# A decoder step on one core: the feed-forward stage's fp32r weight splits replaced by fp16 splits with scales found on the chip

## The chip, the cores and the metric

The kernel runs on one core of one Trainium2 chip. The metric is the device time of one execution in microseconds (us); lower is better. The kernel before takes 1934.26 us, the median of 3 runs (1932.78 to 1934.76).

Five engines of the core matter here. PE multiplies matrices: it holds a block of 128 x 128 weights (loaded by an LDWEIGHTS, shown as PEld) and streams columns of the activations past it into PSUM. DVE, ACT and POOL work element by element. SP only issues DMAs here. Each engine works through its own instructions in a fixed order and waits, where it must, for the others.

## The reference

One step of a one-layer decoder trunk on 256 prompt tokens and 8 x 4 sample tokens, so N = 288 columns; the model width is 2048 (16 blocks of 128, `KT`) and the hidden width of the feed-forward stage is 8192. Only the end of it bears on the change:

```python
mix, st = mixer(xn, states[l], P)
x = x + gt1 * mix
xn = rmsnorm(x, P['g_norm2']) * (1.0 + sc2) + sh2
x = x + gt2 * (jnp.square(jax.nn.relu(xn @ P['w_ff1'])) @ P['w_ff2'])
...
y = rmsnorm(x, g_final)
```

`sh2`, `sc2` and `gt2` are pieces of `mod = silu(c) @ w_ada + b_ada`, one row for the prompt and one for each of the 8 samples (9 columns). All of it is float32, and the weights come from HBM as float32.

## The kernel before

Activations lie transposed: features on the 128 partitions, the 288 tokens along the row. Every large product (the input projection, the branches, `wout`, `wf1`, `wf2`) goes through one generator, `stream` (L151). A weight matrix is cut into blocks of output columns (512 wide); each block is read in tiles of 128 x 1024 floats (512 KB, two row groups of 128 by 512 columns). For each tile:

- SP issues the load of `raw`;
- ACT copies it to `hi`, rounded to fp32r, the type with which PE makes a matmul of 4-byte numbers in one pass (L159);
- DVE makes `lo = raw - hi` (L161);
- PE runs, for each 128 x 128 piece, three matmuls with 288 moving columns: hi by xh, hi by xl and lo by xh (L168), where xh and xl are the same split of the activations. That is 24 matmuls per tile.

A block accumulates in four PSUM banks and is then evacuated by the function `evac` that the caller gives.

The feed-forward stage runs over 8 hidden blocks `hb` of 1024 features. `ff1(hb)` (L1752) makes 1024 hidden features from all 2048 inputs: 2 blocks of `wf1` with 16 row groups each, so 192 matmuls per block of 512 columns. Each result goes through Relu on ACT (L1757), a square on POOL (L1758) and a split into hi and lo on ACT and DVE (L575, L576). `ff2(hb)` (L1764) multiplies these 1024 features with their rows of `wf2`: 4 blocks of 96 matmuls, added to `facc` by DVE (L1774); with hb 6 and 7 the residual with `gt2` follows (L1692 to L1697). The order in the program is ff1(0), then for each hb: ff1(hb+1), ff2(hb). So what ff1(hb+1) makes is not needed by the block that PE does right after it, but four blocks later. Together the stage has 6144 matmuls of 288 columns.

Ahead of it stands a norm: the `wout` blocks end, `every("")` finishes leftovers of the adaLN product (L300), the sum of squares becomes `rs` (L536, L557 to L561), and a loop over 16 features (L1740 to L1746) makes xh2 and xl2: DVE scales (L1740), ACT rounds (L1741, L1744), DVE and POOL subtract.

The remaining adaLN work (`gt2`) runs beside the stage in an order given by a string, `every("E L . L ...")`: at each step of `run` a letter loads, transforms or multiplies one unit of `wada`. Its matmuls have 32 stationary columns (L300 plain fp32, L361 fp16 on scaled parts); four of them use the four column groups of the array at once.

Instructions that are issued under `tc.high_priority()` are put ahead of others on their engine, and a scheduler fixes the order of each engine when the program is built.

Of the kernel before, what the change touches and what calls it, by code (L numbers as in the profile page):

```python
# [8 lines left out]
F32 = mybir.dt.float32  # L9
# [45 lines left out]
def trunk(ctx, tc, io):  # L55
# [22 lines left out]
    def slot(i, dt=F32):  # L78
        return big.tile([P, 8, N], dt, tag=f"s{i}", name=nm(f"s{i}"))
# [28 lines left out]

    ones = cp.tile([P, P], F32, tag="ones", name="ones")
    V.memset(ones, 1.0)  # L110
    eps = cp.tile([P, 1], F32, tag="eps", name="eps")
    V.memset(eps, EPS)

# [37 lines left out]
    def stream(w, blk, act, kt, evac, g0=0, width=512, ahead=True, k0=0, kg=2, behind=None, banks=None):  # L151

        nm_t = width // P
        pss = banks or [pm.tile([P, 512], F32, tag="mm", name=nm("mm")) for _ in range(nm_t)]
        for g in range(k0 // kg, kt // kg):
            with tc.high_priority() if ahead else nullcontext():
                raw, hi, lo = (t.rearrange("p (k m) -> p k m", k=kg) for t in weight_tiles())
                Q.dma_start(raw, w[blk, g0 + g].rearrange("p (k m) -> p k m", k=kg))
                pace["hi"] = S.activation(hi, raw, AF.Copy)  # L159
                with tc.issue_after(behind.ins) if behind and g == 0 else nullcontext():  # L160
                    pace["lo"] = V.tensor_tensor(out=lo, in0=raw, in1=hi.bitcast(F32), op=ALU.subtract)  # L161

            def part(m, kk, i):
                k = kg * g + kk
                ps, ms = pss[m][:, :N], slice(m * P, (m + 1) * P)
                xh, xl = act(k)
                w, x = ((hi, xh), (hi, xl), (lo, xh))[i]
                pace["last"] = T.matmul(ps, w[:, kk, ms], x, start=k == k0 and i == 0, stop=k == kt - 1 and i == 2)  # L168

            if behind and g == 0:  # L170
                for i in range(3):
                    for kk in range(kg):
                        for m in range(nm_t):
                            with tc.issue_after(pace["last"].ins) if pace["last"] else nullcontext():
                                part(m, kk, i)
                yield
                continue
            if behind and g == 1:
                for m in range(nm_t):
                    for kk in range(kg):  # L180
                        for i in range(2):
                            with tc.issue_after(pace["last"].ins):
                                part(m, kk, i)
            for m in range(nm_t):
                for kk in range(kg):
                    for i in range(2 if behind and g == 1 else 0, 3):
                        part(m, kk, i)
                if g == kt // kg - 1:
                    with tc.high_priority():
                        evac(m, pss[m][:, :N])  # L190
            yield


# [1514 lines left out]
    for b in range(4):  # L1708
        def ev_o(m, p, b=b):
            k = 4 * b + m  # L1710
            x = x2[k // 8][:, k % 8, :]
            resid(x, p, GT1, k)
            if k == KT - 1:
                with tc.high_priority(), tc.issue_after(pace["last"].ins):
                    visit(4)
                with tc.issue_after(pace["prod"].ins):
                    sumsq(pss, x, k, ssum)
                with tc.high_priority(), tc.issue_after(pace["sum"].ins):
                    visit()
            else:  # L1720
                sumsq(pss, x, k, ssum)
            if k == KT - 4:
                S.activation(sc([P, 1], "warm", 1), ssum[:, 0:1], AF.Sqrt)
        if b == 3:
            drain("sm1")
            xf.extend((slot(6), slot(7)))
# [6 lines left out]
    xh2 = big.tile([P, KT, N], F32R, tag="xh", name="xh2")  # L1733
    xl2 = big.tile([P, KT, N], F32R, tag="xl", name="xl2")
    with tc.high_priority():
        for k in range(KT):
            f = row(("ar", "mr")[k % 2])
            E = V if k < 2 else G
            h, l, sh = xh2[:, k, :], xl2[:, k, :], mod[:, SH2, k, 0:1]
            V.tensor_tensor(out=f, in0=xf[k // 8][:, k % 8, :], in1=rs, op=ALU.mult)  # L1740
# [4 lines left out]
            V.scalar_tensor_tensor(l[:, 0:NP], f[:, 0:NP], sh, h[:, 0:NP].bitcast(F32), ALU.add, ALU.subtract)  # L1745
            E.tensor_tensor(out=l[:, NP:N], in0=f[:, NP:N], in1=h[:, NP:N].bitcast(F32), op=ALU.subtract)  # L1746


    facc = (slot(6), slot(7))
    pss = None  # L1750

    def ff1(hb):  # L1752
        hh, hl = slot(hb % 2, F32R), slot(2 + hb % 2, F32R)
        for b in range(2):
            def ev(m, p, b=b):
                r = t288()
                S.activation(r, p, AF.Relu)  # L1757
                G.tensor_tensor(out=r, in0=r, in1=r, op=ALU.mult)  # L1758
                i = 4 * b + m
                split(hh[:, i, :], hl[:, i, :], r)  # L1760
            run(stream(io["wf1"], 2 * hb + b, ahead=hb + b > 0, act=lambda k: (xh2[:, k, :], xl2[:, k, :]), kt=KT, evac=ev))
        return hh, hl

    def ff2(hb, h):  # L1764
        for b in range(4):
            def ev(m, p, b=b):
                k = 4 * b + m
                a = facc[k // 8][:, k % 8, :]
                if hb == 0:
                    S.copy(a, p)  # L1770
                    return
                x = x2[k // 8][:, k % 8, :]
                if hb < 7:
                    V.tensor_tensor(out=a, in0=a, in1=p, op=ALU.add)  # L1774
                    if hb == 6:
                        resid(x, a, GT2, k)
                    return
                resid(x, p, GT2, k)
# [3 lines left out]
            run(stream(io["wf2"], b, lambda k: (h[0][:, k, :], h[1][:, k, :]), 8, ev, g0=4 * hb))  # L1782

    h = ff1(0)
    at.update(raw=(None, None, 8))
    slots.update(ids=(9, None, "st"), n=0)
    high.update(ids=(None,))
    every("E L . L . L . . C C C C C C C C C C C C V . .")
    for hb in range(8):
        hn = ff1(hb + 1) if hb < 7 else None  # L1790
        if hb == 6:
# [134 lines left out]
```

## Time and profile before

| what | value |
|---|---|
| median of 3 runs | 1934.26 us |
| span of the profiled execution (first to last instruction) | 1929.9 us |
| feed-forward stage, first to last L168 matmul | 1093.16 to 1915.3 us |
| PE busy over the span | 99% |
| DVE, ACT, POOL busy over the span | 59%, 48%, 12% |
| mean granted clock of TensorE | 0.998 |

The profiled execution's own time is not listed beside its span; the median of the runs is 4.4 us longer than the span, and these 4.4 us are taken as what lies around it. In a row of the groups, "L161 DVE ... x448 | 553.5, 1237" means 448 instructions of line 161, busy for 553.5 us together, 1237 ns each. A row of the timeline gives start, length and a number of neighbouring instructions of one form. For pipelined matmuls the length of one (about 290 ns) is a latency; what PE can do is read from start to start.

### The profile page before, as it was taken

How to read it: one execution, taken by the hardware profiler on the slowest of the kernel's cores; microseconds unless marked ns; L12 is line 12 of the kernel's file. 1: busy time of each engine (PE TensorE's matmuls, PEld its weight loads, DVE VectorE, ACT ScalarE, POOL GpSimd, SP SyncE). 2: the span in 40 equal slices, each digit the busy share in tenths (PEclk: the TensorE clock that was granted, in tenths of full speed). 3: DMA queues.
4: the chain of work that ended last, by engine and by line, in shares of the span. 5: the costliest groups of instructions: out<-in, count | busy, mean ns of one | idle time of the engine just before them, and what ended most of it. 6: DMA issues, size and time to landing. Idle time of an engine off the chain costs nothing.

```text
span 1929.9 us, 37907 instructions
## 1 busy us (share of the span) xinstructions
PE 1902.8 (99%) x15792; PEld 1834.5 (95%) x15792; DVE 1135.2 (59%) x1833; ACT 922.9 (48%) x1361; POOL 238.5 (12%) x315
## 2 busy tenths in 40 slices
PE   8999999999999999999999999999999999999997
PEld 7998888999999999999999999999999999999997
DVE  4677746545684457776478756456454444454565
ACT  5333464444455344566377547465333333343433
POOL 0002100001141000011113521010000000000101
PEclk9999999999999999999999999999999999999999
DMA  9998756547744369856787564654444445444442
GB/s 388 394 367 313 249 197 235 208 161 269 257 154 159 132 217 313 302 186 242 282 349 280 186 243 147 241 198 161 164 167 167 165 154 181 167 165 165 162 169 111
DMA packets 113436, 422.85 MB, mean 219 GB/s; under 512 B 11808, under 2 KB 12096, under 8 KB 110064
## 3 DMA queue, kind: packets, MB, share of 16 engines
q1 hardware_dynamic: 97040, 361.04, 52.5%
q0 software_dynamic: 11472, 42.79, 6.3%
q10 hardware_dynamic: 4752, 16.60, 2.1%
q8 instruction: 124, 2.03, 0.4%
q14 instruction: 48, 0.39, 0.1%
HBM read 403.56 MB, written 16.81 MB: 218 GB/s over the span
## 4 chain that ended last, share of the span: by engine, by line
PE 93%; DVE 4%; DMA 1%; ACT 1%; issue 1%; DVEq 0%; POOL 0%; ACTq 0%; POOLq 0%
PE mm L168 82%; PE pa L300 3%; PE px L168 2%; DVE lo L161 1%; DMA raw<-win 1%; PE pa L361 1%; DVE s L728 0%; PE px L1577 0%; ACT hi L159 0%; PE pi L1560 0%; PE px L1095 0%; PE px L1491 0%; DMA s<-x 0%; PE px L817 0%; DVE s L672 0%
## 5 line engine op out<-in xcount | busy, mean ns | idle before, releaser
L161 DVE TENSOR_TENSOR lo<-raw,hi 128x1024 fp32r<-128x1024 f32 x448 | 553.5, 1237 | 486.3 <-ACT hi L159 465.9
L159 ACT ACTIVATE hi<-raw 128x1024 fp32r<-128x1024 f32 x448 | 473.7, 1059 | 700.7 <-PE mm L168 537.8
L168 PE MATMUL mm<-xh,hi 128*128 128x288 f32 x2464 | 725.9, 299 | 4.1 <-ACT xh L646 1.7
L168 PE MATMUL mm<-xl,hi 128*128 128x288 f32 x2464 | 722.8, 296 | 0.0
L168 PE MATMUL mm<-xh,lo 128*128 128x288 f32 x2464 | 706.6, 295 | 2.0 <-DVE lo L161 1.9
L168 PE MATMUL mm<-s,hi 128*128 128x288 f32 x3328 | 655.9, 296 | 1.1 <-DVE s L1697 0.7
L168 PEld LDWEIGHTS mm<-s,hi 128*128 128x128 f32 x3328 | 527.1, 188 | 5.3 <-issue 3.1
L168 PEld LDWEIGHTS mm<-xh,hi 128*128 128x128 f32 x2464 | 460.3, 188 | 17.0 <-issue 8.6
L168 PE MATMUL mm<-s,lo 128*128 128x288 f32 x1664 | 471.1, 295 | 1.6 <-DVE lo L161 1.0
L168 PEld LDWEIGHTS mm<-xl,hi 128*128 128x128 f32 x2464 | 462.3, 188 | 1.4
L168 PEld LDWEIGHTS mm<-xh,lo 128*128 128x128 f32 x2464 | 456.6, 188 | 4.9 <-DVE lo L161 2.9
L168 PEld LDWEIGHTS mm<-s,lo 128*128 128x128 f32 x1664 | 306.5, 188 | 2.3 <-DVE lo L161 2.1
L161 DVE TENSOR_TENSOR lo<-s,hi 128x1024 fp32r<-128x1024 f32 x80 | 98.0, 1224 | 102.6 <-ACT hi L159 102.6
L159 ACT ACTIVATE hi<-s 128x1024 fp32r<-128x1024 f32 x80 | 84.8, 1061 | 127.3 <-PE mm L168 124.0
L1758 POOL TENSOR_TENSOR t<-t 128x288 f32<-128x288 f32 x64 | 64.4, 1020 | 637.2 <-ACT t L1757 637.2
L1774 DVE TENSOR_TENSOR s<-s,mm 128x288 f32<-128x288 f32 x96 | 40.0, 449 | 28.4 <-PE mm L168 27.4
L1258 POOL TENSOR_TENSOR s<-s,t 128x288 f32<-128x288 f32 x16 | 22.6, 1441 | 169.3 <-DVE t L1257 135.9
L576 DVE TENSOR_TENSOR s<-t,s 128x288 fp32r<-128x288 f32 x64 | 32.4, 546 | 15.5 <-ACT s L575 15.5
L575 ACT ACTIVATE s<-t 128x288 fp32r<-128x288 f32 x64 | 27.5, 442 | 25.6 <-POOL t L1758 25.6
L300 PE MATMUL pa<-s,silc 128*32 128x128 f32 (+2 forms) x768 | 33.9, 322 | 1.0 <-DMA s<-wq 1.0
L300 PEld LDWEIGHTS pa<-s,silc 128*32 128x32 f32 x768 | 22.4, 115 | 9.8 <-issue 6.6
L168 PE MATMUL px<-xh,hi 128*128 128x288 f32 x96 | 28.3, 300 | 0.0
(473 smaller groups left out, 1477.0 us busy)
## 6 DMA issues: line engine op xcount, KB each, us to landing
raw<-win SPq DMA_DIRECT2D x192, 512.0 KB, 4.5
raw<-wf SPq DMA_DIRECT2D x176, 512.0 KB, 4.3
s<-wf SPq DMA_DIRECT2D x80, 512.0 KB, 3.5
s<-wq SPq DMA_DIRECT2D x20, 1024.0 KB, 9.8
raw<-wout SPq DMA_DIRECT2D x32, 512.0 KB, 5.8
s<-wada SPq DMA_DIRECT2D x13, 1024.0 KB, 7.6
ag<-wada POOLq DMA_DIRECT2D x12, 1024.0 KB, 7.5
ag<-wada SPq DMA_DIRECT2D x11, 1024.0 KB, 6.5
```

The source lines that it names most:

```text
L159: pace["hi"] = S.activation(hi, raw, AF.Copy)
L161: pace["lo"] = V.tensor_tensor(out=lo, in0=raw, in1=hi.bitcast(F32), op=ALU.subtract)
L168: pace["last"] = T.matmul(ps, w[:, kk, ms], x, start=k == k0 and i == 0, stop=k == kt - 1 and i == 2)
L300: pace["prod"] = T.matmul(ps[32 * j:32 * j + 32, h * w // 4:(h + 1) * w // 4], stat(k), v[:, j], start=k == 0 and h == 0, stop=k == kt - 1 ...
L361: pace["prod"] = T.matmul(ps[32 * j:32 * j + 32, a:a + 256], c, v[:, j], start=q == i == n == 0, stop=q == KT // each - 1 and n == 1, skip ...
L575: S.activation(dst_h[:, r], src[:, r], AF.Copy)
L576: V.tensor_tensor(out=dst_l[:, r], in0=src[:, r], in1=dst_h[:, r].bitcast(F32), op=ALU.subtract)
L1258: (V if br == 1 else G).tensor_tensor(out=a, in0=a, in1=t, op=ALU.add)
L1758: G.tensor_tensor(out=r, in0=r, in1=r, op=ALU.mult)
L1774: V.tensor_tensor(out=a, in0=a, in1=p, op=ALU.add)
```

## The change

In the feed-forward stage only, `stream` is replaced by `stream_half`, which works with fp16:

- **The scale of a block.** Each block has 4 raw tiles and 96 matmuls. ACT squares each raw tile with a running sum per partition (L235), PE adds the 128 partitions by a small matmul with ones (L238), and DVE turns the sum into powers of two u and t by integer arithmetic on the exponent (`power_of_two`, four instructions on 128 x 1, L198 to L201), then `c = t * back` (L241).
- **The split.** hi = u times raw, rounded to fp16, by ACT for every other tile (L247) and by DVE for the others (L249); lo = u times raw minus hi, in fp16, by DVE (L250). The matmuls (L258) are all fp16.
- **The blocks.** `wf1` comes in 256-wide blocks, so ff1 has 4 blocks of 96 matmuls where it had 2 of 192.
- **The activations.** x is scaled through SC2 and SH2 (ahead of the last `wout` block) and split into fp16 (`x16`). In ff1 the evacuation is Relu with scale c on ACT (L1841) and a square on ACT with row sums (L1842); POOL has nothing left to do there. At the end of ff1 the row sums go through ACT (L1847), a matmul with ones (L1849) and `power_of_two`, and only then is the hidden block split into fp16, in four pieces of 128 x 576 on ACT (L1854) and DVE (L1855).
- **The evacuation of ff2** multiplies by c (L1871).
- **Buffers.** 11 raw tiles in rotation (three of them `raw`, four parts of one tile `xl`, two of `s8`, two of `s3`) and 6 pairs of hi and lo. The string of `every` is spaced anew.

The core of the diff (line numbers of the changed kernel are those named above):

```diff
+    def power_of_two(p, n, of):
+        q, t, u = (of[:, i:i + 1] for i in (4, 5, 6))
+        V.tensor_reduce(out=q, in_=p[:, 0:n], axis=AX.X, op=ALU.add)
+        V.tensor_scalar(q.bitcast(I32), q.bitcast(I32), 0x7F000000, 1, ALU.bitwise_and, ALU.logical_shift_right)
+        V.tensor_scalar(u.bitcast(I32), q.bitcast(I32), -1, 204 << 23, ALU.mult, ALU.add)
+        V.tensor_scalar(t.bitcast(I32), q.bitcast(I32), 50 << 23, None, ALU.add)
+        return t, u
...
+    def stream_half(w, blk, act, kt, evac, back, g0=0, width=512):
...
+        with tc.high_priority():
+            for g in range(n):
+                raw = half_raw()
+                Q.dma_start(raw, w[blk, g0 + g])
+                pace["hi"] = S.activation(junk, raw, AF.Square, accum_out=of[:, g:g + 1])
+                raws.append(raw)
+            p = misc()
+            T.matmul(p[:, 0:n], words(ones, 1, BF16), words(of[:, 0:n], 1, BF16), start=True, stop=True)
+            t, u = power_of_two(p, n, of)
+            c = of[:, 7:8]
+            V.tensor_tensor(out=c, in0=t, in1=back, op=ALU.mult)
+        for g in range(n):
+            with tc.high_priority():
+                hi, lo = half_pair()
+                half["n"] += 1
+                if half["n"] % 2:
+                    pace["hi"] = S.activation(hi, raws[g], AF.Copy, scale=u)
+                else:
+                    V.tensor_scalar(hi, raws[g], u, None, ALU.mult)
+                pace["lo"] = V.scalar_tensor_tensor(lo, raws[g], u, hi, ALU.mult, ALU.subtract)
...
+    half["raw"] = ["raw", "raw", "raw"] + [("xl", i, 64) for i in range(4)] + [("s8", i, 32) for i in range(2)] + [("s3", i, 32) for i in range(2)]
...
     def ff1(hb):
-        hh, hl = slot(hb % 2, F32R), slot(2 + hb % 2, F32R)
-        for b in range(2):
-            def ev(m, p, b=b):
+        h = slot(2)
+        rows = sc([P, 8], "lam6", 1)
+        for b in range(4):
+            def ev(m, p, c, b=b):
+                i = 2 * b + m
                 r = t288()
-                S.activation(r, p, AF.Relu)
-                G.tensor_tensor(out=r, in0=r, in1=r, op=ALU.mult)
-                i = 4 * b + m
-                split(hh[:, i, :], hl[:, i, :], r)
+                S.activation(r, p, AF.Relu, scale=c)
+                S.activation(h[:, i, :], r, AF.Square, accum_out=rows[:, i:i + 1])
...
+        with tc.high_priority():
+            hof = sc([P, 8], "hs", 2)
+            q = hof[:, 0:1]
+            S.activation(rows, rows, AF.Square, accum_out=q)
+            p = misc()
+            T.matmul(p[:, 0:1], ones, q, start=True, stop=True)
+            back, u = power_of_two(p, 1, hof)
+            hx = big.tile([P, 2, 8, N], F16, tag=f"s{hb % 2}", name=nm("hx"))
+            for i in range(0, 8, 2):
+                r = slice(i, i + 2)
+                S.activation(hx[:, 0, r], h[:, r], AF.Copy, scale=u)
+                V.scalar_tensor_tensor(hx[:, 1, r], h[:, r], u, hx[:, 0, r], ALU.mult, ALU.subtract)
+        return hx, back
```

The order of the instructions is the same before and after until just ahead of the last `wout` block. Two engines are shown behind it, both at the end of one ff1, where ff2's first block begins.

PE before, the last matmuls of an ff1 (stationary hi or lo, moving xh2 or xl2) and the first of the ff2 that follows (moving s0 and s2, the hidden block made earlier):

```order
L168 MATMUL mm_2469_18077<-xl2_12669,hi_2492_18289 128x288
L168 MATMUL mm_2469_18077<-xh2_12668,lo_2493_18290 128x288
L168 MATMUL mm_2498_18338<-s0_2302_16766,hi_2503_18343 128x288
L168 MATMUL mm_2498_18338<-s2_2303_16767,hi_2503_18343 128x288
L168 MATMUL mm_2498_18338<-s0_2302_16766,lo_2504_18344 128x288
```

PE after, the same place (px: a PSUM bank for the small sums; hs: the row sums of the hidden block; sums: the sums of a block's raw tiles; x16: the scaled activations; lo_2360 and hi_2374 are pairs of hi and lo halves):

```order
L258 MATMUL mm_2352_18451<-x16_12678,lo_2360_18551 128x288
L1849 MATMUL px_2364_18586<-hs_2363_18584,ones_87 128x1
L238 LDWEIGHTS ones_87
L238 MATMUL px_2373_18616<-sums_2370_18605,ones_87 128x4
L238 LDWEIGHTS ones_87
L238 MATMUL px_2386_18751<-sums_2382_18739,ones_87 128x4
L258 LDWEIGHTS hi_2374_18623
L258 MATMUL mm_2366_18601<-hx_2260_17461,hi_2374_18623 128x288
```

Where one block's matmuls ran into the next one's, three sums now stand between them: that of the hidden block just finished, and behind it those of the next two blocks of weights. The other seven ends of an ff1 read the same.

DVE before, at the same place: the lo parts of the last tiles of ff1 and of the first tiles of ff2 (lo_2504 is the first that ff2 uses), with the splits of the hidden block (s3) among them:

```order
L161 TENSOR_TENSOR lo_2490_18260<-s8_2488_18258,hi_2489_18259 128x1024
L161 TENSOR_TENSOR lo_2493_18290<-raw_2491_18288,hi_2492_18289 128x1024
L161 TENSOR_TENSOR lo_2504_18344<-raw_2502_18342,hi_2503_18343 128x1024
L161 TENSOR_TENSOR lo_2507_18374<-s8_2505_18372,hi_2506_18373 128x1024
L576 TENSOR_TENSOR s3_2433_17809<-t288_2494_18300,s1_2432_17808 128x288
L161 TENSOR_TENSOR lo_2510_18404<-raw_2508_18402,hi_2509_18403 128x1024
```

DVE after, from the moment the next block's scale u is known (a pair, hi half and lo half, is one buffer here, and the buffers are called hi and lo in turn: hi_2374 is the pair that ff2's first matmuls use, lo_2375, lo_2377 and lo_2388 are other pairs of the next two blocks; L249 writes a pair's hi half, L250 its lo half):

```order
L249 TENSOR_SCALAR lo_2377_18704<-s3_2372_18613,sums_2370_18605 128x1024
L200 TENSOR_SCALAR sums_2382_18739<-sums_2382_18739 128x1
L201 TENSOR_SCALAR sums_2382_18739<-sums_2382_18739 128x1
L241 TENSOR_TENSOR sums_2370_18605<-sums_2370_18605,hs_2258_17453 128x1
L1855 SCALAR_TENSOR_TENSOR hx_2365_18592<-s2_2312_18045,hs_2363_18584,hx_2365_18592 128x576
L250 SCALAR_TENSOR_TENSOR lo_2375_18650<-s8_2371_18608,sums_2370_18605,lo_2375_18650 128x1024
...
L250 SCALAR_TENSOR_TENSOR lo_2377_18704<-s3_2372_18613,sums_2370_18605,lo_2377_18704 128x1024
L249 TENSOR_SCALAR lo_2388_18785<-raw_2383_18742,sums_2382_18739 128x1024
L241 TENSOR_TENSOR sums_2382_18739<-sums_2382_18739,hs_2258_17453 128x1
...
L250 SCALAR_TENSOR_TENSOR hi_2374_18623<-xl_2355_18456,sums_2370_18605,hi_2374_18623 128x1024
```

The lo part that ff2 needs first (the last row) moved behind those of other pairs, and behind three of the four pieces of the hidden block's split (L1855; two of them are at the "..." marks). Ahead of the first row shown stand ten small instructions of three `power_of_two` and one more L249. ACT's order there is: Relu and square of ff1's last results (L1841, L1842), in seven of the eight places one more L235, then L1847, three L1854, and the L247 of pair hi_2374.

More of the change, by code (lines that the diff above doesn't have):

```diff
@@ new lines, in trunk, with half_raw, half_pair @@
+    half = {"raw": [], "pair": [], "r": 0, "p": 0, "n": 0}
+    parted = {}
+    def half_raw():
+        i = half["raw"][half["r"] % len(half["raw"])]
+        half["r"] += 1
+        if i in ("raw", "lo"):
+            return wp.tile([P, 1024], F32, tag=i, name=nm(i), bufs=3)
+        tag, n, of = i
+        if n == 0:
+            parted[tag] = flat(big.tile([P, of // 4, N], F32, tag=tag, name=nm(tag)))
+        return parted[tag][:, 1024 * n:1024 * n + 1024]
+    def half_pair():
+        i = half["pair"][half["p"] % len(half["pair"])]
+        half["p"] += 1
+        t = wp.tile([P, 2048], F16, tag=i, name=nm(i), bufs=3)
+        return t[:, 0:1024], t[:, 1024:2048]
@@ L1725, in trunk @@
             drain("sm1")
+            xof = sc([P, 8], "xs", 1)
+            q2 = xof[:, 0:2]
+            for i, (kind, f) in enumerate(((SC2, 64.0), (SH2, 2.0))):
+                S.activation(junk[:, 0:9 * KT], modf[:, 9 * KT * kind:9 * KT * (kind + 1)], AF.Square, scale=f, accum_out=q2[:, i:i + 1])
+            p = misc()
+            T.matmul(p[:, 0:2], ones, q2, start=True, stop=True)
+            xback, u = power_of_two(p, 2, xof)
+            r = modf[:, 9 * KT * SH2:9 * KT * (SC2 + 1)]
+            V.tensor_scalar(r, r, u, None, ALU.mult)
             xf.extend((slot(6), slot(7)))
```

49 lines of the change are left out of this document (35 added, 14 removed).

## The prediction

> **What bounds the kernel now.** I read the page first. One engine is busy nearly all the time, at full granted clock, and the matmuls of L168 carry it; the splits of L159 and L161 fill half of ACT and DVE.
>
> ```profile
> span 1929.9 us, 37907 instructions
> PE 1902.8 (99%) x15792; PEld 1834.5 (95%) x15792; DVE 1135.2 (59%) x1833; ACT 922.9 (48%) x1361; POOL 238.5 (12%) x315
> PEclk9999999999999999999999999999999999999999
> L161 DVE TENSOR_TENSOR lo<-raw,hi 128x1024 fp32r<-128x1024 f32 x448 | 553.5, 1237 | 486.3 <-ACT hi L159 465.9
> raw<-wf SPq DMA_DIRECT2D x176, 512.0 KB, 4.3
> ```
>
> Next the same counts for the feed-forward stage alone (columns: busy time of PE, PEld, DVE, ACT, POOL, then clock, DMA share, GB/s), and the longest waits in it.
>
> ```profile
> 1093.10:1908.00 814.90, 814.90 (x6220) 813.63 (x6217) 434.80 (x597) 368.86 (x512) 87.22 (x103) 1.00 0.49 172
> POOL t L1758 <- ACT t L1757: 637.2, 42, 72.9
> ACT hi L159 <- PE mm L168: 396.6, 202, 4.9
> DVE lo L161 <- ACT hi L159: 329.6, 200, 4.2
> ```
>
> PE is busy 814.90 of 814.90 us; the others wait for PE, never PE for them. So the stage lasts 6144 matmuls times their spacing. The first row below, of the chain of waits, is where the stage's first matmul starts; the second, of the timeline, is its last; the other two give the spacing:
>
> ```profile
> 1093.16 36.94 PE mm L168 x277
> ...
> 1915.32 0.29 PE L168 MATMUL mm<-s,lo 128*128 128x288 f32 x1
> ```
>
> ```profile
> 1395.46 0.29 PE L168 MATMUL mm<-xl,hi 128*128 128x288 f32 x1
> ...
> 1396.39 0.29 PE L168 MATMUL mm<-xh,lo 128*128 128x288 f32 x1
> ```
>
> Seven spacings in 0.93 us are 133 ns; 6144 x 133.3 = 819 us, which is the stage (1093.16 to 1915.3 less some adaLN products). DVE has 380 us to spare there, ACT 446.
>
> **The fp16 matmul.** The trace has no fp16 matmul of this shape. It has fp16 with 32 stationary columns and 256 moving ones, four to a group, and plain fp32 of the same shape:
>
> ```profile
> 637.66 0.29 PE L361 MATMUL pa<-uh,uc 128*32 128x256 f16 x4
> ...
> 638.00 0.28 PE L361 MATMUL pa<-st,uc 128*32 128x256 f16 x4
> 241.76 1.13 PE L817 MATMUL px<-s,s 128*128 128x288 f32 x4
> L817 PE MATMUL px<-s,s 128*128 128x288 f32 x32 | 9.6, 409 | 0.0
> ```
>
> Three spacings of L361 are 0.34 us: 113 ns for 256 columns, 127.5 for 288 in proportion. L817's four are spaced (1.13 - 0.41)/3 = 0.240 us, 1.8 times an fp32r matmul; read as two passes, a pass takes 120 ns. So fp32r runs about a tenth behind what the array can do. I take 122.5 ns, nearer L817, which has our shape: 6144 x 10.8 = **66.4 us gained**; at 127.5 it would be 35.6, at 133 nothing.
>
> **What the change adds all along.** Their nearest rows:
>
> ```profile
> L339 ACT ACTIVATE uh<-s 128x1024 f16<-128x1024 f32 x14 | 14.6, 1041 | 0.0
> L339 ACT ACTIVATION_READ_ACCUMULATOR uh<-s 128x1 f32 x14 | 2.6, 187 | 0.0
> L345 ACT ACTIVATE uh<-s,ue 128x1024 f16<-128x1024 f32 x14 | 15.9, 1136 | 0.8 <-DVE ue L342 0.6 <-DVE s L1697 0.2
> L347 DVE SCALAR_TENSOR_TENSOR s<-s,ue,uh 128x1024 f16<-128x1024 f32 x14 | 20.2, 1442 | 1.5 <-ACT uh L345 1.3
> L1598 DVE TENSOR_SCALAR s<-s,gn 128x288 f32<-128x288 f32 x8 | 2.9, 364 | 0.0
> L1740 DVE TENSOR_TENSOR row<-s,row 128x288 f32<-128x288 f32 x16 | 6.9, 459 | 0.3
> 1327.99 1.22 DVE L161 TENSOR_TENSOR lo<-s,hi 128x1024 fp32r<-128x1024 f32 x1
> 1329.13 0.15 DVE L340 TENSOR_SCALAR ue<-ue 128x1 int32<-128x1 int32 x1
> 1329.31 0.15 DVE L341 TENSOR_SCALAR ue<-ue 128x1 f32<-128x1 f32 x1
> L1757 ACT ACTIVATE t<-mm 128x288 f32<-128x288 f32 x64 | 24.7, 399 | 5.9 <-PE mm L168 5.9
> L1774 DVE TENSOR_TENSOR s<-s,mm 128x288 f32<-128x288 f32 x96 | 40.0, 449 | 28.4 <-PE mm L168 27.4
> 700.47 0.53 PE L1538 MATMUL px<-csm,mks 128*128 128x32 f32 x4
> 700.83 0.38 PE L168 MATMUL mm<-xl,hi 128*128 128x288 f32 x1
> ```
>
> A Square with its sum (L235) is priced by L339 plus its read, 1.23 us, some 1.13 from start to start; L247 by L345; L250 by L347, 1.44 us long and, since neighbours on DVE overlap by about 0.1 us (1327.99 to 1329.13 for 1.22), 1.34 from start to start. L249 isn't in the trace. TENSOR_TENSOR goes from 459 ns at 288 elements to 1237 at 1024, so 1.06 ns per element and 155 ns fixed; L1598 with the same 155 has 0.73 per element, which gives L249 0.90 us. The Trainium skill, page "VectorE: DVE Perf Modes", section "Mode 2×_2P", says that an op with one fp32 source from SBUF runs at two elements a cycle where one with two tensors runs at one; L249 would then be about 0.70 us by an estimate from that rule and the row of L161. L1598 bears out the direction, not the full factor.
>
> A block of PE is 96 x 0.1225 = 11.76 us. DVE needs in an ff2 block 2 x 0.8 + 4 x 1.34 + 5 x 0.185 + 4 x 0.40 = 9.5 us; ACT 4 x 1.13 + 2 x 1.1 and the evacuations or hidden splits, 8 to 9 us. Both fit, but DVE's slack falls from half to a fifth: this work lies beside PE and costs nothing while its order is right. POOL's square goes; POOL idled 637 us there, so nothing is gained. Loads keep their bytes and PE's block is 8% shorter, so 172 GB/s becomes about 187: no bound. Of the 64 small sums (L238, one a block) 16 lie at the ends of ff1, below; the other 48 take PE about 0.09 us each by L1538 (four in the 0.36 us from 700.47 to the next L168 at 700.83): **+4.3**. Third blocks wait a little for the loads that the four-part tile xl lets through late, and DVE does `gt2`'s residuals in hb 6: **+5** (0 to 10). The scaling of SC2 and SH2 stands on PE 45 matmuls behind the sums that it needs: 6 us of cover, no cost.
>
> **The eight ends of ff1: a new wait of PE.** PE's order decides. Behind ff1's last matmul stands L1849, which waits for ff1's last evacuation; queued behind it, though they need nothing of it, are the L238 of the next two blocks; and all of ff2's matmuls need a pair scaled by that L238. Counted from the start of ff1's last matmul, in us:
>
> - matmul ends 0.29; Relu (399 ns) 0.74; Square and read (430 and 187 ns by L543 and L339's kin) 1.33; the extra L235 2.45; L1847, some 0.2 us on 8 elements, and its read 2.83; L1849 and the L238 behind it 3.25.
> - DVE: ten small instructions at 0.185, 5.1; two L249, 6.8; three small, 7.35; then L1855, L250, L1855, L250, L249, L241, L1855 and the needed L250. L1855 (576 elements) is 0.65 by this row:
>
> ```profile
> L1653 DVE SCALAR_TENSOR_TENSOR s<-s,s 128x576 f32<-128x576 f32 x4 | 3.0, 749 | 0.0
> L543 ACT ACTIVATE t<-s 128x288 f32<-128x288 f32 x15 | 6.0, 435 | 6.8 <-DVE s L1697 6.7
> ```
>
> - 3 x 0.65 + 3 x 1.34 + 0.85 + 0.18 = 7.0, so the first lo half is there at 14.35.
>
> ACT has that pair's hi at about 7 to 8 (three L1854, then L247), so PE does 8 matmuls with hi alone, 1 us, and waits again. Lost: 14.35 - 0.13 - 1.0 = 13.2; with L249 at 0.6 from start to start 12.5. I take 13.0: 8 x 13.0 = **104 us** (11.5 to 15.5 each, 92 to 124). Behind the wait on PE lies everything; on SP the loads whose raw tiles come free only after it, so no load fills the gap.
>
> **The start of the stage.** The fourth raw tile of ff1(0)'s first block lies in xl, which L300 reads until about 1091.4; a load takes 4.3 us, so with Square, sum and split the first matmul comes near 1099.9 where it came at 1093.16. DVE must, besides, make the x chain:
>
> ```profile
> 1089.50 1.93 PE L300 MATMUL pa<-xl,silc 128*32 128x256 f32 x32
> 1091.30 0.83 DVE L1740 TENSOR_TENSOR row<-s,row 128x288 f32<-128x288 f32 x2
> 1114.64 0.48 DVE L1745 SCALAR_TENSOR_TENSOR xl<-row,mod,xh 128x256 fp32r<-128x256 f32 x1
> ```
>
> That chain runs to 1114.6 already; with 5 L249 and 10 L250 in place of its L161 the first two blocks end near 1129.5 instead of 1093.1 + 192 x 0.1225 = 1116.6: **+13** (10 to 17).
>
> **The clock.** PE will now stand still for several us at a time. The trace shows what that does at the two ends of the program.
>
> ```profile
> 7.39 1.93 PE L300 MATMUL pa<-s,silc 128*32 128x128 f32 x32 [0.62 <-DMA s<-wq]
> 14.71 1.08 PE L300 MATMUL pa<-s,silc 128*32 128x128 f32 x32 [0.42 <-DMA s<-wq]
> 1918.20:1921.35 3.15, 0.08 (x1) 0.00 (x0) 2.52 (x5) 0.31 (x1) 0.00 (x0) 1.00 0.00 0
> 1921.35:1930.00 8.65, 0.00 (x0) 0.00 (x0) 4.22 (x7) 0.00 (x0) 0.00 (x0) 0.50 0.69 273
> ```
>
> The same 32 matmuls take 1.93 us at 7.39 and 1.08 at 14.71: half speed until PE had worked up to 7 us. At the end the granted clock falls to 0.50 some 3.2 us after PE stops. So each end of ff1 can cost 0 to 3.5 us more, half the stretch at half speed. I take 2.0, the middle, since DVE still paces the first matmuls then: 8 x 2.0 = **+16** (0 to 28). The Trainium skill speaks against the change here: "TensorE: Matmul & The Clock Gate", Part 1, says that one idle window of about 3.4 us drops the array to half its clock and a busy one restores it. By it the estimate is 1.7 us per gap, 14 in all, and the sum 2 us lower; the tail row agrees with the drop, the start row shows a slower return.
>
> **Sum.** 1929.9 - 66.4 + 4.3 + 5 + 104 + 13 + 16 = 2005.8 us of span; the median of the runs is 4.4 above the span (1934.26 against 1929.9), so **2010 us**.
>
> **Rivals.**
> - *The ends of ff1 are covered* (faster). The mechanism: DVE is quick enough on 2-byte results. It decides at 1934.3 - 66.4 + 4.3 + 5 + 13 = 1890.2, so 44 us, or 5.5 per end with no clock loss. For: L249 and L250 write half the bytes. Against: L347 writes fp16 already and takes 1442 ns, and the evacuation with the small instructions alone takes 5.1 us before any split. At 4 us per end: 1890 + 32 = 1922. Chance 0.07.
> - *fp16 is spaced like fp32r*, 133 ns: the change doesn't do what it says. For: PE loads new weights for every matmul and PEld is busy 95%. Against: L817 and L361. 2010 + 66 = 2076. Chance 0.10.
> - *DVE becomes the bound of every block*: its 9.5 us plus late starts exceed 11.76 by, say, 0.7 in all 64 blocks: +45, 2055. For: DVE's chain also holds the scale's small instructions, queued behind splits. Against: the sum of busy times. Chance 0.08.
> - The forecast, with its own range of 1974 to 2050 from the bounds: 0.75.
>
> **How the numbers follow.** The low end takes the short gaps with no clock loss and an early start, 1934.3 - 66.4 + 4.3 + 92 + 10 = 1974, a little less for unknown prices: 1968. The high end holds the third rival and the slow ends of the terms, 2062; the second rival and the first lie outside (0.17). Faster by over 0.2% (3.9 us, about what a measurement here can tell from none): 0.07; within it 0.02; slower 0.91.
>
> **What would show it.** Right: eight gaps of 12 to 15 us between the last L258 of an ff1 and the next steady L258, with L1849 and two L238 in them and DVE without a pause; L258 spaced 122 ns in between; the first L258 near 1100; PE's clock at half behind the gaps. Wrong: L238 ready before L1849 and no gap; a spacing of 133; gaps at every block.

## The result, and the profile after

The changed kernel takes 1988.93 us (median of 4 runs, 1987.26 to 1991.3), the kernel before in the same runs 1933.52 (1932.07 to 1934.76): a ratio of 1.0286, 95% interval 1.0271 to 1.0301. The change makes the kernel slower, by 55 us; the forecast was 2010, 76 us slower.

The page of the kernel after, its first lines. PE is no longer busy all the time, and in the last half of the 40 slices its share and its granted clock both fall below nine tenths in turn:

```profile
span 1988.1 us, 38811 instructions
PE 1875.1 (94%) x15874; PEld 1632.7 (82%) x15874; DVE 1261.1 (63%) x2290; ACT 1119.6 (56%) x1861; POOL 174.9 (9%) x251
PE   8999999999999999999999788989889898989897
PEclk9999999999999999999999888989989898989899
```

PE's waits in the stage, from behind the first ff1 on (columns: who waited for whom, us in total, times, longest). Before there was no line of PE in this view:

```profile
PE mm L258 <- ACT hi L247: 31.3, 9, 4.3
PE px L1849 <- ACT lam L1847: 20.8, 8, 5.0
PE mm L258 <- DVE hi L250: 19.5, 8, 3.0
PE px L238 <- DVE hs L198: 1.8, 8, 0.2
```

A fifth line, two waits for L1871 with 1.3 us in all, is left out. Eight times each (the first line nine, two of them at one end), at the eight ends of ff1: 73.4 us in which PE stands still. The timeline of PE at one of them (start, length, count, and in brackets the idle time and what ended it):

```profile
1216.62 0.78 PE L258 MATMUL mm<-x,lo 128*128 128x288 f16 x5
1219.79 0.38 PE L1849 MATMUL px<-hs,ones 128*128 128x1 f32 x2 [2.39 <-ACT lam L1847]
1220.03 0.16 PE L238 MATMUL px<-sums,ones 128*128 128x4 bf16 x1
1220.42 0.16 PE L238 MATMUL px<-sums,ones 128*128 128x4 bf16 x1 [0.22 <-DVE hs L198]
1224.15 2.10 PE L258 MATMUL mm<-hx,hi 128*128 128x288 f16 x8 [3.56 <-ACT hi L247]
1229.24 3.06 PE L258 MATMUL mm<-hx,hi 128*128 128x288 f16 x12 [2.99 <-DVE hi L250]
```

The last matmul of ff1 starts at 1217.1, the matmuls run on from 1229.2: 12.1 us, with eight matmuls on hi alone between. DVE's timeline in the same place:

```profile
1220.21 0.16 DVE L198 TENSOR_REDUCE hs<-px 128x1 f32<-128x1 f32 x1 [17.00 <-PE px L238]
...
1221.07 1.41 DVE L249 TENSOR_SCALAR lo<-raw,sums 128x1024 f16<-128x1024 f32 x2
...
1222.59 0.81 DVE L1855 SCALAR_TENSOR_TENSOR hx<-s,hs,hx 128x576 f16<-128x576 f32 x1
1223.32 1.28 DVE L250 SCALAR_TENSOR_TENSOR lo<-raw,sums,lo 128x1024 f16<-128x1024 f32 x1
1224.51 0.81 DVE L1855 SCALAR_TENSOR_TENSOR hx<-s,hs,hx 128x576 f16<-128x576 f32 x1
...
1227.90 1.28 DVE L250 SCALAR_TENSOR_TENSOR hi<-s,sums,hi 128x1024 f16<-128x1024 f32 x1
```

DVE has nothing to do for 17 us and then works without a pause; the lo half that PE needs comes last of all these (the last row). Between the ends the matmuls run as fast as the change promised. In a timeline of the steady part:

```profile
1270.09 2.37 PE L258 MATMUL mm<-hx,lo 128*128 128x288 f16 x18
L258 PE MATMUL mm<-hx,lo 128*128 128x288 f16 x1536 | 209.8, 288 | 0.0
```

Eighteen matmuls in 2.37 us, 0.288 for one: 17 spacings of 122.5 ns, and a steady block of 96 takes 11.76 to 11.81 us from start to start. Times between the starts of the blocks, counted from the trace, show where the 55 us are. (A block is counted here from the last matmul before it to its own last one.) The eight blocks behind an ff1 take 23.4 to 27.0 us, 200 together where 94 would do: **106 us lost**. The first ff1 ends 63.5 us after 1093.16, where 384 x 0.1225 = 47.0 would do: **16.5 lost**. All else together (sums, residuals, adaLN products) is 5.7 us. The stage gains 66.4 by the spacing. Of the 5.7 us some 3.3 are adaLN products that stand in the stage before the change too, so the balance is 106 + 16.5 + 5.7 - 3.3 - 66.4 = 58.5 us. The two profiled spans differ by 58.2, the medians of the runs by 55.4.

The clock at the end shown above (the columns are busy time of PE, PEld, DVE, ACT, POOL, then clock, DMA share, GB/s):

```profile
1217.00:1220.00 3.00, 0.61 (x6) 0.31 (x4) 0.00 (x0) 2.56 (x9) 0.00 (x0) 1.00 0.01 3
1220.00:1223.00 3.00, 0.36 (x4) 0.13 (x3) 2.73 (x16) 2.83 (x6) 0.00 (x0) 0.72 0.00 0
1223.00:1226.00 3.00, 1.85 (x8) 1.03 (x8) 3.00 (x4) 3.00 (x5) 0.00 (x0) 0.50 0.00 0
...
1232.00:1235.00 3.00, 3.00 (x15) 1.86 (x14) 2.92 (x6) 2.26 (x4) 0.00 (x0) 0.50 1.02 416
1235.00:1240.00 5.00, 5.00 (x43) 4.01 (x42) 4.02 (x9) 3.26 (x6) 0.00 (x0) 1.00 0.43 174
```

It falls to one half within the pause, and comes back near 1235.0, 5.7 us after the matmuls run on; at the eight ends that takes 2.7 to 5.7 us by the clock record of the trace. In the whole stage the trace has 25 us of extra spacing (240 ns in place of 122.5) from this, 22 of them at the eight ends; the other 3 us lie at the start, where the clock stands at one half from 1098.4 to 1112.1.

### The profile page after: what moved, and what is told of

It is laid out like the page before. It is cut to its first block, busy times and chain, and to the rows that moved or that the text cites. A ratio compares the mean times of both kernels' runs of the same rounds, so it can differ in the third digit from the quotient of the medians.

```text
span 1988.1 us, 38811 instructions
## 1 busy us (share of the span) xinstructions
PE 1875.1 (94%) x15874; PEld 1632.7 (82%) x15874; DVE 1261.1 (63%) x2290; ACT 1119.6 (56%) x1861; POOL 174.9 (9%) x251
## 4 chain that ended last, share of the span: by engine, by line
PE 84%; DVE 7%; issue 3%; ACT 3%; DMA 3%; SPq 0%; POOL 0%; DVEq 0%; ACTq 0%; POOLq 0%
PE mm L169 37%; PE mm L258 36%; PE pa L371 3%; PE px L169 1%; DVE lo L162 1%; DMA raw<-win 1%; DVE lo L249 1%; DVE lo L250 1%; ACT con L235 1%; DVE hi L250 1%; DMA raw<-wf 1%; DVE hx L1855 1%; PE pa L432 0%; ACT hi L160 0%; DVE s L799 0%
## 5 line engine op out<-in xcount | busy, mean ns | idle before, releaser
L162 DVE TENSOR_TENSOR lo<-raw,hi 128x1024 fp32r<-128x1024 f32 x272 | 334.7, 1232 | 251.9 <-ACT hi L160 231.5
L258 PEld LDWEIGHTS <-hi 128*128 128x128 f16 x3072 | 306.9, 101 | 157.8 <-ACT hi L247 42.2
L169 PE MATMUL mm<-xh,hi 128*128 128x288 f32 x1440 | 428.7, 301 | 5.0 <-ACT xh L717 1.6
L169 PE MATMUL mm<-xl,hi 128*128 128x288 f32 x1440 | 423.0, 296 | 0.0
L169 PE MATMUL mm<-xh,lo 128*128 128x288 f32 x1440 | 412.0, 296 | 2.0 <-DVE lo L162 1.9
L258 PEld LDWEIGHTS <-lo 128*128 128x128 f16 x3072 | 299.7, 98 | 77.3 <-issue 0.2
L258 PE MATMUL mm<-hx,hi 128*128 128x288 f16 x1536 | 226.1, 302 | 45.7 <-ACT hi L247 26.1
L169 PE MATMUL mm<-s,hi 128*128 128x288 f32 x1280 | 254.2, 298 | 1.0 <-DVE s L1768 0.7
L258 PE MATMUL mm<-x,hi 128*128 128x288 f16 x1536 | 206.6, 291 | 13.2 <-ACT hi L247 8.5
L258 PE MATMUL mm<-hx,lo 128*128 128x288 f16 x1536 | 209.8, 288 | 0.0
L169 PEld LDWEIGHTS mm<-s,hi 128*128 128x128 f32 x1280 | 203.0, 189 | 5.1 <-issue 2.7
L258 PE MATMUL mm<-x,lo 128*128 128x288 f16 x1536 | 200.3, 286 | 0.0
L169 PE MATMUL mm<-s,lo 128*128 128x288 f32 x640 | 179.6, 296 | 1.6 <-DVE lo L162 1.6
L235 ACT ACTIVATE con<-xl 128x1024 bf16<-128x1024 f32 x92 | 96.7, 1051 | 49.8 <-DMA xl<-wf 31.6
L235 ACT ACTIVATE con<-s 128x1024 bf16<-128x1024 f32 x92 | 96.7, 1051 | 46.0 <-DMA s<-wf 18.5
L198 DVE TENSOR_REDUCE hs<-px 128x1 f32<-128x1 f32 x8 | 1.3, 158 | 140.1 <-PE px L238 140.1
L235 ACT ACTIVATE con<-raw 128x1024 bf16<-128x1024 f32 x72 | 75.8, 1052 | 17.4 <-DVE s L1871 6.9
```

The costliest lines, as they stand in the source:

```text
L198: V.tensor_reduce(out=q, in_=p[:, 0:n], axis=AX.X, op=ALU.add)
L235: pace["hi"] = S.activation(junk, raw, AF.Square, accum_out=of[:, g:g + 1])
L258: pace["last"] = T.matmul(ps, a[:, kk, ms], x, start=k == 0 and i == 0, stop=k == kt - 1 and i == 2)
```

## The experiments

The theory behind the forecast: at each end of ff1 the small sums of the next blocks (L238) are queued on PE behind L1849, which waits for ff1's last evacuation, so scale, split and matmul follow one another with PE idle. The main rival: DVE has more to do at the ends than it can, whatever the order on PE.

**1. The sums of the next blocks traced ahead of the end of ff1.** All work stays; the loads, squares and L238 of the next two blocks are written ahead of the hidden block's sum:

```diff
+        ready = [first(hb - 1, last, b) for b in range(2)]
         with tc.high_priority():
             hof = sc([P, 8], "hs", 2)
...
-            run(stream_half(io["wf2"], b, ..., 8, ev, back, g0=4 * hb))
+            run(stream_half(io["wf2"], b, ..., 8, ev, back, g0=4 * hb, head=head[b] if b < len(head) else None))
```

> The two next blocks' loads, squares and sums of squares are traced ahead of the end of ff1, so that their L238 stand in front of L1849 on PE; all work stays. Theory (the sums of the next blocks are queued behind L1849): the eight first blocks after an ff1, 25.0 us each now, come to 12 to 13.5 us, no half-speed matmuls are left behind them, so about 1989 - 98 = 1891 us (1880 to 1910), faster than the kernel before. Rival (DVE has too much to do at the end of ff1, whatever PE's order): DVE's list of some 8 us stays in the way, 1950 or more.

Measured: 1888.63 us (1887.72 to 1891.07), a ratio to the kernel before of 0.9767 (0.9753 to 0.9782). PE's waits of 0.2 us and more from 1140 to 1900, all of them, and PE at the same end of ff1 (L264 is its matmul, L236 its sum of a block's squares):

```profile
PE mm L264 <- ACT t L1852: 1.8, 1, 1.8
PE mm L264 <- DVE s L1883: 0.9, 3, 0.3
```

```profile
1200.77 2.49 PE L264 MATMUL mm<-x,lo 128*128 128x288 f16 x19
1203.10 0.41 PE L264 MATMUL mm<-hx,hi 128*128 128x288 f16 x2
1203.34 0.17 PE L236 MATMUL px<-sums,ones 128*128 128x4 bf16 x1
1203.37 2.12 PE L264 MATMUL mm<-hx,hi 128*128 128x288 f16 x16
```

The matmuls on x run into those on hx without a pause, and seven of the eight blocks behind an ff1 take 11.9 to 13.0 us (one takes 13.9). DVE does the same work, so the rival falls. The time lies in the range that the theory gave, and this version beats both kernels.

**2. Only the split of the hidden block later.** L1849 stays where it was; L1854 and L1855 go behind the next block's second tile (and the tile h, which they read, is taken later to allow that):

```diff
-            for i in range(0, 8, 2):
-                r = slice(i, i + 2)
-                S.activation(hx[:, 0, r], h[:, r], AF.Copy, scale=u)
-                V.scalar_tensor_tensor(hx[:, 1, r], h[:, r], u, hx[:, 0, r], ALU.mult, ALU.subtract)
+        def split_h():
+            with tc.high_priority(), tc.issue_after(pace["lo"].ins), tc.issue_after(pace["hi"].ins):
+                ...
+        late.append(split_h)
```

> Only the split of the hidden block (L1854, L1855) is moved behind the second tile of the next block; L1849 stays ahead of the L238. Theory: DVE reaches the needed lo half three L1855 (0.73 each) and perhaps an L250 (1.2) earlier, ACT the hi half earlier too, so 2 to 3 us less at each of eight ends: about 1969 us (1962 to 1975). Rival (the split is DVE's overload at the ends, and with it gone the wait goes): under 1930. Rival (the list is not what PE waits for): 1989.

Measured: 1961.63 us (1961.11 to 1963.52), 27 less than the changed kernel, 0.4 under the range given. The waits in the same stretch:

```profile
PE px L1857 <- ACT lam L1855: 21.1, 8, 5.2
PE mm L258 <- ACT hi L247: 15.6, 8, 2.5
PE mm L258 <- DVE hi L250: 10.6, 8, 2.1
```

The first wait, for the hidden block's sum, is what it was (20.8). The two behind it are half as long, 24.6 us less together. So as long as the sums stand behind L1849, the order of DVE's and ACT's work behind them is worth a quarter of the loss. The two shares don't add up to the whole: experiment 1 takes nearly all of the loss away, and it takes nothing out of DVE's or ACT's work.

**3. PE kept at work in the pauses.** Nothing moves; idle matmuls, whose results nobody reads, fill two of the three holes (`pad` is 26 for the second of the two blocks behind an end):

```diff
+            with tc.issue_after(pace["last"].ins):
+                dummies(18)
             p = misc()
             T.matmul(p[:, 0:1], ones, q, start=True, stop=True)
...
+            if pad:
+                with tc.issue_after(behind.ins):
+                    dummies(pad)
```

> At each end of ff1 PE gets 18 idle matmuls of the same shape ahead of L1849 and 26 behind the second L238, whose results nobody reads; they fill 2.2 of 2.7 us and 3.2 of 3.6 us in which PE stands still now, and nothing else moves. Theory (the half-speed matmuls behind the ends are the clock gate's answer to the pause, and cost their whole length): granted clock stays 1.00 there, 25.1 us of slow spacing go, 1989 - 20 to 25 = 1964 to 1969 us. Rival (those matmuls wait for DVE's pairs anyway): 1985 to 1992, with the clock up.

Measured: 1975.8 us (1974.12 to 1976.17), 13 less: between the theory's range and the rival's. In the trace the extra spacing at half speed falls from 25.1 to 13.3 us, by 11.8. PE at the same end of ff1 (L267 is the matmul, L229 the idle one), and the windows:

```profile
1215.70 3.35 PE L229 MATMUL pi<-x 128*128 128x288 f16 x26
1218.88 1.14 PE L267 MATMUL mm<-hx,hi 128*128 128x288 f16 x8
1223.76 2.96 PE L267 MATMUL mm<-hx,hi 128*128 128x288 f16 x16 [3.73 <-DVE hi L259]
```

```profile
1218.00:1221.00 3.00, 2.02 (x17) 1.37 (x14) 3.00 (x4) 3.00 (x5) 0.00 (x0) 1.00 0.00 0
1221.00:1224.00 3.00, 0.24 (x2) 0.21 (x3) 3.00 (x5) 3.00 (x6) 0.00 (x0) 1.00 0.00 0
1224.00:1227.00 3.00, 3.00 (x19) 2.02 (x17) 3.00 (x4) 0.38 (x1) 0.00 (x0) 0.65 0.70 235
1227.00:1230.00 3.00, 3.00 (x21) 2.20 (x20) 3.00 (x4) 2.27 (x4) 0.00 (x0) 0.78 1.00 395
```

The eight matmuls on hi now take 1.14 us where they took 2.10, and the clock holds there through the first two holes. The third, 3.7 us for the lo half, was not filled, and it alone still brings the clock down to 0.65 and 0.78. So the half-speed matmuls are the answer to the pause, as the theory has it. Their length is lost only where DVE is not waited for behind them: for the eight on hi the rival is mostly right, since the third hole grew from 2.99 to 3.73 us when they became shorter by 0.96. The expected 20 to 25 us took no account of the third hole. Filling that one too was not tried.

**4. The scales of the weights as constants.** No L235, L238 nor their `power_of_two`; u = 64 and t = 1/64 stand in place of the scales found, so the numbers are rounded at another place:

```diff
-                pace["hi"] = S.activation(junk, raw, AF.Square, accum_out=of[:, g:g + 1])
                 raws.append(raw)
-            p = misc()
-            T.matmul(p[:, 0:n], words(ones, 1, BF16), words(of[:, 0:n], 1, BF16), start=True, stop=True)
-            t, u = power_of_two(p, n, of)
+            t, u = fixed_scale
```

> The scales of the weights are constants (64 and 1/64) in place of L235, L238 and their power_of_two; the scale of the hidden block with L1847 and L1849 stays. Theory: without a sum behind L1849 the pairs of the next block are ready ahead of the end of ff1, the first blocks come to 12 to 13 us, and the start comes earlier by the squares and sums, 3 to 5 us; the 48 other sums cost 3 us: about 1989 - 98 - 7 = 1884 us (1870 to 1900). Rival (DVE's pairs and the hidden split are what PE waits for): 1940 or more.

Measured: 1879.56 us (1878.36 to 1882.59), ratio 0.9721 (0.9706 to 0.9735). With the sums in a good order (experiment 1) finding the scales on the chip therefore costs about 9 us in 1880. Most of it lies at the start: the first ff1 ends at 1149.8 us here and at 1155.7 there.

**5. The start: another order of the raw tiles.** On top of experiment 1, so that the first block needs no part of xl:

```diff
-    half["raw"] = ["raw", "raw", "raw"] + [("xl", i, 64) for i in range(4)] + [("s8", i, 32) ...] + [("s3", i, 32) ...]
+    half["raw"] = ["raw", "raw", "raw"] + [("s8", i, 32) ...] + [("s3", i, 32) ...] + [("xl", i, 64) for i in range(4)]
```

> The kernel with the sums of the next blocks ahead of L1849 (1888.6 us), and the raw tiles in another order of rotation, so that the stage's first block takes three raw and one of s8 in place of a part of xl, which is still read by the adaLN product. Theory (the first matmul waits for the load into xl): the first matmul of the stage comes near 1094 in place of 1101.7, but the x chain and the splits on DVE go on pacing the first block, so only 3 to 6 us come off: 1883 to 1886 us. Rival (DVE's x chain alone paces the start): 1887 to 1890. Second rival (the start is all the wait for xl): 1880 or less.

Measured: 1887.88 us (1886.62 to 1888.7), ratio 0.9759 (0.9746 to 0.9772) against 0.9767 in experiment 1: no difference, which is the range of the first rival and not of the theory. PE there:

```profile
1096.86 0.66 PE L264 MATMUL mm<-x,hi 128*128 128x288 f16 x4 [2.18 <-ACT hi L253]
1100.11 0.16 PE L236 MATMUL px<-sums,ones 128*128 128x4 bf16 x1 [2.59 <-ACT con L233]
1100.62 2.10 PE L264 MATMUL mm<-x,hi 128*128 128x288 f16 x8 [0.34 <-DVE hi L256]
```

The first matmul comes 4.9 us earlier (1096.86 against 1101.73), and the first block takes 21.3 us where it took 18.6; the first ff1 ends at 1155.9 against 1155.7. The wait for xl was covered by something else. The first row is the changed kernel between 1102 and 1120 us, the second the one with constant scales:

```profile
1102.00:1120.00 18.00, 13.76 (x86) 9.39 (x87) 17.07 (x31) 14.87 (x32) 8.21 (x14) 0.72 0.48 181
```

```profile
1102.00:1120.00 18.00, 16.93 (x122) 12.53 (x122) 15.48 (x27) 8.91 (x21) 7.42 (x19) 0.91 0.84 329
```

With the scales found on the chip DVE is busy 17.1 of 18 us there and ACT 14.9; with constants ACT has 8.9 and PE gets 16.9 us of work in. Which of the two engines decides is not shown by this: in the changed kernel ACT is busy 13.5 of the 13.7 us from 1098.4 to 1112.1 and DVE 11.8, and the waits that PE has in experiment 5 up to 1160 us name ACT for 7.1 us, POOL for 1.5 and DVE for 0.3.

**6. The start: some of the x chain on POOL.** On top of experiment 5:

```diff
-            V.tensor_tensor(out=f, in0=xf[k // 8][:, k % 8, :], in1=rs, op=ALU.mult)
+            (G if k % 4 == 3 else V).tensor_tensor(out=f, in0=xf[k // 8][:, k % 8, :], in1=rs, op=ALU.mult)
```

> As the one before, and of the x chain ahead of the stage every fourth multiplication by rs (k % 4 == 3, on DVE 0.37 us from start to start) goes to POOL. Theory (DVE paces the first block): 4 x 0.37 = 1.5 us less work on DVE, 1 to 2 us off. Rival (POOL takes 1 us for it and delays its feature): 0 to 2 us more.

Measured: 1890.98 us (1888.41 to 1893.01), ratio 0.9774 (0.9758 to 0.979) against 0.9759: no gain, but 3 us more, where the theory gave 1 to 2 less and the rival up to 2 more; the intervals overlap. So 1.5 us less work on DVE did not shorten the start, and that DVE alone paces it is not confirmed.

**7. All hi halves on DVE.** On top of experiment 1:

```diff
-                if half["n"] % 2:
-                    pace["hi"] = S.activation(hi, raws[g], AF.Copy, scale=u)
-                else:
-                    V.tensor_scalar(hi, raws[g], u, None, ALU.mult)
+                V.tensor_scalar(hi, raws[g], u, None, ALU.mult)
```

> The kernel with the sums of the next blocks ahead of L1849 (1888.6 us), with all hi halves made by DVE (four L249 a block in place of two), so DVE has in an ff2 block 4 x 0.67 + 4 x 1.20 + 5 x 0.1 + 4 x 0.43 = 9.7 us of PE's 11.76. Theory (DVE has that room): the steady blocks stay at 11.8 us, and only the start and the blocks behind ff1 with the hidden split grow: 1890 to 1900 us. Rival (DVE is at its bound already): every block grows by a us or more, 1940 or more.

Measured: 1892.6 us (1891.15 to 1894.73), ratio 0.9785 (0.9771 to 0.9799). A stretch of the stage in it:

```profile
1440.00:1500.00 60.00, 60.00 (x496) 47.92 (x495) 51.37 (x87) 34.61 (x71) 0.00 (x0) 1.00 0.52 189
```

DVE is busy 51.4 of 60 us and PE still has no gap: DVE's load is no bound in the steady part, as the theory has it.

**8. The block width alone.** The kernel before, fp32r and all, with `wf1` in 256-wide blocks (`range(4)` in ff1, `width=256, kg=4`).

> The kernel before, with wf1 in 256-wide blocks (four of 96 matmuls an ff1) and nothing else: fp32r, no scales. Theory (the width alone costs PE nothing once the stage runs): spacing stays at 133 ns and the time within 0.3% of 1934, with at most some 5 us at the start, where a block of half the width uses each feature of the x chain up in half the time. Rival (the narrow blocks are part of the loss at the ends of ff1): 1945 or more.

Measured: 1938.11 us (1936.85 to 1939.65), ratio 1.0024 (1.0015 to 1.0033), 3 to 6 us more. PE's waits at the start of the stage, all of 0.2 us and more up to 1130, where the kernel before had none:

```profile
PE mm L168 <- POOL xl L1746: 1.1, 2, 0.8
PE mm L168 <- ACT xh L1744: 0.2, 1, 0.2
PE mm L168 <- ACT hi L159: 0.2, 1, 0.2
```

Half of the width uses each feature of the x chain up in half the time, so PE overtakes the chain. These waits are 1.5 us. Counted from the starts in the trace, the first ff1 is 3.9 us longer (1095.05 to 1150.08 against 1093.09 to 1144.21), and all that follows it in the stage only 0.6. So the narrow blocks cost something at the start alone, and nothing at the later ends of ff1: the rival falls. (The remaining 2.0 us of the profiled execution lie ahead of the stage.)

**9. One word: another PSUM bank.** Why did the sums stand behind L1849 at all? The pool px has two banks, and they are given out in the order of the program: that of L1849 comes ahead of those of the next blocks. Here L1849 takes the bank of the norms, and nothing else is changed:

```diff
-            p = misc()
+            p = longp()
             T.matmul(p[:, 0:1], ones, q, start=True, stop=True)
```

> The changed kernel with one word changed: the sum of the hidden block (L1849) is written to the PSUM bank that serves the norms, idle in this stage, in place of one of the two px banks that the sums of the weight blocks rotate through. In the order of PE the L238 of the next two blocks then stand tens of matmuls ahead of L1849, and L1849 about 15 matmuls into the next block. Theory (the two px banks, given out in program order, put the sums behind L1849): as with the sums traced first, 1884 to 1894 us. Rival (px was not what held them, and the tracing order alone did it): 1960 or more.

Measured: 1893.61 us (1892.1 to 1896.61), ratio 0.9788 (0.9772 to 0.9803). PE at the end of ff1 shown above:

```profile
1200.23 2.74 PE L258 MATMUL mm<-x,lo 128*128 128x288 f16 x21
1202.81 0.41 PE L258 MATMUL mm<-hx,hi 128*128 128x288 f16 x2
1203.05 0.17 PE L238 MATMUL px<-sums,ones 128*128 128x4 bf16 x1
1203.08 2.12 PE L258 MATMUL mm<-hx,hi 128*128 128x288 f16 x16
```

The same order as in experiment 1, and the same lack of a pause, by one word. The 5 us between the two are one block: the second behind the ff1 that ends near 1395 takes 18.7 us here and 11.8 there. PE waits in it for DVE's evacuations (L1871, 2.6 us), and 2.4 us more are half-speed spacing, since the clock falls to one half from 1411.4 to 1418.2 behind these short waits.

## Why the prediction was right, point by point

The sign, the mechanism and its place were right, and 1988.93 lies in the range of 1968 to 2062. The forecast of 2010 was 21 us too slow, and the terms show why.

- *The fp16 matmul*, 122.5 ns and 66.4 us: right to the digit the trace gives (17 spacings in 2.08 us; steady blocks of 11.76 to 11.79 us). The plain fp32 row of the same shape was the better guide, the 32-column fp16 row (127.5) the worse one. That a record of that row is two passes was assumed, and no run here shows it, so the hit to the digit is in part luck.
- *The ends of ff1*, 104 us and 16 for the clock: 106 in all where 120 were forecast; experiments 1 and 9 show that this is the order on PE. Of the 106 us 22 are the clock, so the stall proper is 84, 10.5 at each end, where 13.0 was taken: the term was 20 us too high, and the clock's was 6 too low, so that the two errors cancel in part. The pauses from ff1's last matmul to the steady ones are 11.2 to 14.9 us long, where 12 to 15 was named as the sign of being right. The walk had the needed lo half at 14.35 us after the last matmul of ff1; it came at 12.1. Ten small instructions took 0.86 us (1220.21 to 1221.07) and not 1.85, since three chains that don't depend on one another (hs and the sums of two blocks) run interleaved; the rows of L340 and L341 that priced them were one chain. The large ones, in the page's groups after:

```profile
L249 DVE TENSOR_SCALAR lo<-xl,sums 128x1024 f16<-128x1024 f32 x46 | 34.5, 749 | 13.2 <-PE mm L258 12.8 <-issue 0.4
L250 DVE SCALAR_TENSOR_TENSOR hi<-xl,sums,hi 128x1024 f16<-128x1024 f32 x46 | 58.8, 1281 | 28.7 <-ACT hi L247 28.1
L1855 DVE SCALAR_TENSOR_TENSOR hx<-s,hs,hx 128x576 f16<-128x576 f32 x32 | 25.5, 812 | 0.0
```

  L250 is 1.28 us where L347's 1.44 stood for it, L1855 0.81 where L1653's 0.75 did. L249 is 0.75: the 0.90 worked out from L1598 was too long. The estimate from the rule of the Trainium skill, page "VectorE: DVE Perf Modes", section "Mode 2×_2P", was 0.70, and the measured row is nearer to that.
- *The clock*, 2.0 us at each end: 22 us in all, 2.8 each, inside the bounds of 0 to 3.5. The pause brings the clock to one half as the tail of the kernel before had shown, and experiment 3 shows that the pause is the cause. The estimate of 1.7 us a gap was half of the one busy window of about 3.4 us that, by the Trainium skill, page "TensorE: Matmul & The Clock Gate", Part 1, restores the clock. The trace has more: the eight matmuls between the holes run at half speed as well, and behind the last hole the clock comes back only after 2.7 to 5.7 us.
- *The start*, 13 us: 16.5. The size was near, one of the two reasons was wrong: experiment 5 took the wait for xl away and gained nothing. What covered that wait is only narrowed down: without the squares and sums (experiment 4) the first ff1 ends 5.9 us earlier, with less work on DVE (experiment 6) nothing is gained, and ACT, which the forecast left out here, is as full as DVE. About 3 of the 16.5 us are half-speed spacing, which the forecast counted at the eight ends alone. And 1.0 us of it the profiled execution had lost within the first 200 us of the program, where both kernels do the same.
- *Sums, loads and residuals*, 9.3 us: 5.7, and in these are about 3.3 us of adaLN products that the kernel before had as well. The small sums slip in between matmuls almost free: steady blocks with one take 0 to 0.05 us over 11.76.
- *What lies around the span*, 4.4 us: this was misread. The median of the runs is 0.8 above the profiled span this time, but each run's own time is 1.7 to 1.9 us above its own span wherever both are on record (1989.89 against 1988.1 for the profiled run). So the 4.4 held some 2.6 us by which the profiled execution before was faster than the median, and the one after was 1.0 slower than its median. That is spread between executions and no effect of the change.
- *The rivals.* fp16 spaced like fp32r: excluded by the spacing. DVE as the bound of every block: excluded by experiment 7. The ends covered: not so in this kernel, but it is what experiments 1 and 9 make of it.

With 14 us less at the ends, 7 less in the rest (9.3 and 3.3 against 5.7), 3.5 more at the start and 3.6 less from that spread, the 21 us are accounted for.

## What to carry to other kernels

A faster matmul was gained in full and lost again to a sum of four numbers in the wrong place of PE's queue: where an engine is the bound, look at every small instruction that a change puts into its queue, at what that one waits for, and at what stands behind it that doesn't need to wait. Buffers given out in program order can fix such an order without a line of code saying so; a bank of its own, or tracing the next block's preparation ahead of this block's end, freed 95 to 100 us here. A pause of PE costs its own length and can cost some us at half clock as well, 2.8 at each end here.

## What the runs showed of the hardware that was not expected

- A pause of 3.7 us alone (experiment 3, third hole) brought the granted clock to 0.65 and 0.78 in the two stretches of 3 us behind it. The length alone doesn't decide: at two other ends of that run PE paused for 2.3 us, and the clock fell to one half after one pause (from 1330.7 to 1334.1) and stayed at 1.00 after the other (near 1543). In experiment 9 a row of pauses of at most 1.5 us was enough.
- By the clock record of the trace, the clock stays at one half for 10.2 us at three of the eight ends and for 13.7 at five; in experiment 3 it is 3.4 or 6.8. All of these are multiples of 3.4 us.
- Independent small DVE instructions start 0.06 to 0.12 us apart (ten in 0.86 us, with one wait for PE among them), dependent ones 0.18.
- A small bf16 sum between fp16 matmuls (L238, 168 ns long) delays the row of matmuls by 0.03 us at full clock, where 0.09 was charged from a row amid fp32r matmuls.
